# A two-layer decoder trunk on one core: where the first layer's weight sums are formed, where x's inverse root is computed, and a new order of units

## The chip, the core and the metric

The kernel runs on one core of a Trainium2 chip. The engines that matter are TensorE (PE in the profile; PEld is its weight load), VectorE (DVE), ScalarE (ACT) and GpSimd (POOL). SyncE (SP) and GpSimd issue DMAs. Each engine takes its instructions in the order in which they were emitted. SBUF holds data for all engines; PSUM receives the matmul results. The metric is the device time of one execution in microseconds (us), median of several.

## The reference

Two layers; in each, `h = RMSNorm(x)`, one projection `p = h @ W_in` (1024 to 3488 columns), four head groups on slices of `p`, each gated by a SiLU path, and an output projection added to `x`. All is float32, 512 tokens.

```python
h = rmsnorm(x, norm_g)
p = h @ w_in
(cq, ckv, kr, g_a, c_h, c_b, c_c, g_b, sg_u, sg_v, g_c, mq, mk, mv, g_d) = jnp.split(p, offs, axis=-1)
# A: latent attention from cq, ckv, kr   B: gated short convolution of c_c * c_h, times c_b
# C: sg_u times a causal mix of layernorm(sg_v)   D: block-sparse attention from mq, mk, mv
y = jnp.concatenate([o_a * silu(g_a), o_b * silu(g_b), o_c * silu(g_c), o_d * silu(g_d)], axis=-1)
x = x + y @ w_out
```

Two blocks of columns of `W_in` matter here: "sq" (`sg_v` and `mq`, 512 columns) and "kv" (`mk` and `mv`, 512 columns).

## The kernel before

**Precision.** A float32 product is made of three matmuls: each operand is split into a high part (rounded to the matmul type) and a low part (the rest), and high x high, high x low and low x high are summed in PSUM (`mm3`, L296). So each weight block of 128 x 1024 ("unit", 512 KB) is loaded as `raw`, its high part `whi` is copied from it, mostly on ScalarE, and its low part `wlo = raw - whi` is formed on VectorE from two SBUF tensors (`split_units` L455, `low_half` L497).

**Units and buffers.** All units of a layer are listed in order (`order`, from `SEQ0` for the first layer, L47, and `SEQ1` for the second, L50). `load_units` (L415) issues the loads on SyncE's queue in this order, `split_units` splits them in this order, and `main` (L1766) emits their matmuls. Raw blocks and low parts share a ring of eight buffers (`ringS`); a unit's low part goes to the ring buffer one before its raw block's. High parts have six buffers. A few units take other buffers that lie idle at that time: `hS` (two), `v4S` (four), `ydS` (two, idle until `mq` and `mk` take them, L1401). The first three units (`EARLY`) are split into the space of `yTh` and `yTl`, which is not yet used; in the profile p11's weights are therefore called yTh and yTl, and so are the row sums of the products below.

**Seven products instead of eight.** The token-major sq and kv columns are computed by a Strassen-like scheme: tokens in two halves, the 1024 inner rows in two halves, the columns in sq and kv. The four weight blocks are p11 and p21 (sq), p12 and p22 (kv), each of two units (j = 0, 1). The seven products of `SPROD` are p11, p21, p3, p4, p2, p1, p22; four of them use sums of weight blocks: p3 = p22 + p12, p1 = p12 + p11, p2 = p11 + p3, p4 = p21 + p2. `product` (L1834) emits 24 matmuls per product; p11 and p21 accumulate in the tiles pz, p3 and p4 in px, p2, p1 and p22 in py. `h_first`, `h_sums` and `sum_split` (L912 to L948) form the sums of rows of h that go with them, on VectorE (tiles `a`) with a split on ScalarE and VectorE. `p_out` (L1874) and its users take the results: `sv_chain` and `mqk_chain` for sq, `mqk_chain` and `mv_chain` for kv.

**Weight sums through DRAM.** For both layers the weight sums are formed by DMAs in DRAM (`t_sums`, L372): first eight copies, block to sum buffer, on SyncE's queue; then eight DMAs on GpSimd's queue that add a second block to the copy. Their results are then loaded as units p1 to p4 from `psum_w`. For the first layer this starts at 10 us of the plan (`TSP`), one step each 1.7 us (`PGAP`).

**Root of x.** In the first layer the norm's inverse root is not applied to h but to results. `x_stats` (L803) computes the mean square, at `ROWT` of the plan emits its power -0.5 on GpSimd (`pow_rstd`, L753), and splits it (`xr2`, the tile xr). `x_row` (L826) spreads it on GpSimd into two diagonal matrices (rdh, rdl), multiplies them by ones on PE (rrow), and copies the row to `rh`, by which the gates and features are scaled (`gate` L1223, `from_acc` L1293).

**Order of emission.** `Order` (L85) is a planner in Python: every chain of instructions is a generator, and each instruction is emitted when the planner's clocks of the engines say that its inputs are nearly there. The costs are fixed formulas in `Chain` (L177); GpSimd's is 290 ns plus 2.0 ns per element. Splits of units not yet wanted are held back while ScalarE's or VectorE's clock is more than `WSLACK` ahead. `TS0` is when the weight sums of the output projection and of the second layer start. `SGLOAD` names the product after which the spatial weights are loaded.

Of the kernel before, what the change touches and what calls it, by code (L numbers as in the profile page):

```python
# [29 lines left out]
TWO_PI = 6.283185307179586  # L30

NRING, NW, NT2 = 8, 6, 11
WSLACK = 100.0
AHEAD, URGENT, VSLACK = 4, 2, 300.0
NWARM, FILL, FILLEND = 6, 0.9, 15000.0
MIXT, MIXLAG, ROWT, COLT = 44000.0, 2000.0, 36000.0, 17500.0
KSPLIT, HMEAN = 6, 0.0
PAIRS = {}
LOPRIO = -5
# [4 lines left out]
STOK = (0, 1)  # L44
SPROD = ("p11", "p21", "p3", "p4", "p2", "p1", "p22")
SSUMS = {"p3": 0, "p2": 1, "p1": 2, "p22": 0}
SEQ0 = ['ga0', 'p11', 'p21', 'p3', 'p4', 'ga1', 'p2', 'p1', 'p22', 'ch0', 'su0', 'gc0', 'cc0', 'gd0', 'cb0', 'gd1', 'ch1', 'cc1', 'cb1', 'gb0', 'su1', 'gb1', 'gc1']  # L47
EARLY = [f"{n}{j}_0" if n in SPROD else f"{n}_0" for n in SEQ0[:3] for j in range(2 if n in SPROD else 1)][:3]
EARLYREL = EARLY[2][:-3] if EARLY[2][0] == "p" else EARLY[2][:-2]
SEQ1 = ['p11', 'ga0', 'p21', 'p3', 'p4', 'ga1', 'p2', 'ch0', 'p1', 'p22', 'cc0', 'gd0', 'gd1', 'su0', 'cb0', 'gb0', 'ch1', 'gc0', 'cc1', 'cb1', 'gb1', 'su1', 'gc1']  # L50
K0, K1, KK = (2, 3, 0, 1), (4, 5, 6, 7), (0, 2, 3, 1)
ZPROD = ("b11", "t3", "b21", "t4", "t2", "t1", "b22")
TS0 = 70000.0
NEWT = ((), ())
SUMLAT = 10000.0
HSTART = 'ga0'
FAR = 3
TSP, PGAP = 10000.0, 1700.0
HADD_G = ()
ZHOME = 'ss'  # L60
SGLOAD = ('p2', 'p4')
MLAGO = ('p4', 'p4')
TAIL = ((0, 256), (256, 512))

# [167 lines left out]
def hybrid_trunk(ctx: ExitStack, tc: tile.TileContext, x, positions, norm_g, w_c, w_f, w_t, w_o, mla_q_norm_g,  # L232
# [3 lines left out]
    V, A, G, PE = nc.vector, nc.scalar, nc.gpsimd, nc.tensor  # L236
# [125 lines left out]
    def z_src(l, n, j):  # L362
        return tsum[l, n][j] if n in ("t1", "t2", "t3", "t4") else quad(l, n, j)

    psum_w = {(l, n): dr.tile([2, P, 1024], F32, name=f"{n}_{l}") for l in STOK for n in ("p1", "p2", "p3", "p4")}
    tsum_ev.update({(l, n, j): Event() for l, n in psum_w for j in range(2)})

    def p_src(l, n, j):

        return psum_w[l, n][j] if len(n) == 2 else w_t[l, int(n[2]) - 1, 2 * int(n[1]) - 2 + j]  # L370

    def t_sums(*streams):  # L372

        first = streams[0][0] == 0 and streams[0][2] == "p"
        gap = PGAP if first else 4000.0 if len(streams) == 1 else 3000.0
        steps = [(l, src, t + n, b + x, y[0].replace("b", b).replace("t", t) + y[1:], j)
                 for n, x, y in (("3", "12", "b22"), ("1", "11", "b12"), ("2", "11", "t3"), ("4", "21", "t2"))
                 for l, src, t, b in streams for j in range(2)]
        for l, src, n, x, _, j in steps:
            o.clk["D"] = max(o.clk["D"], o.now) + 1500.0  # L380
            nc.sync.dma_start(src(l, n, j), src(l, x, j))
            yield o.now + gap
        for l, src, n, _, y, j in steps:
            o.clk["G"] = max(o.clk["G"], o.now) + 1000.0
            nc.gpsimd.dma_start(src(l, n, j), src(l, y, j), accum_op=ALU.add, max_dma_last_dim=1024)  # L385
            o.set(tsum_ev[l, n, j], o.now + (SUMLAT if first else 10000.0))
            yield o.now + gap

    FEATS = ["ga0", "ga1", "ch0", "ch1", "cb0", "cb1", "cc0", "cc1", "gb0", "gb1", "su0", "su1",
# [2 lines left out]
    for l in range(DEPTH):  # L392
# [18 lines left out]
        for half in range(2):  # L411
            for kq in WORDER:
                add_unit(w_o[l, half, kq], 2, 512, f"wo{half}{kq}_{l}")

    def load_units():  # L415
        for u in order:
            ch = Chain(o)
            u.raw_slots = ringS[u.idx % NRING]
            if u.name in ("uq_0", "ukv_0"):
                u.raw_slots = hS  # L420
                u.raw = yield from hS.get(ch, f"raw_{u.name}")
            elif u.name in ("p210_0", "p211_0"):
# [12 lines left out]
            key = (int(u.name[-1]), u.name[:-3], ord(u.name[-3]) - 48)
            if key in tsum_ev:
                yield from ch.wait(tsum_ev[key])
            n = u.a * u.b
            if u.name == "c0_0":
                for i in range(2):  # L440
                    sl = slice(i * n // 2, (i + 1) * n // 2)
                    ch = Chain(o)
                    dma(ch, P * n * 2, u.raw[:, sl], u.src[:, sl])
                    o.set(u.landed[i], ch.t)
                    if i == 0:
                        load_xk(1, 2)
            else:
                dma(ch, P * n * 4, u.raw[:, :n], u.src)
                ch.t += LATE.get(u.name, 0.0)
            o.set(u.loaded, ch.t)  # L450
            for e in LOAD_HOOKS.pop(u.name, ()):
                e()
            yield o.now
# [42 lines left out]

    def low_half(u, i, ch, raw, hi, g, whole):  # L497
        if u.lo is None and i == 0:
            u.lo = yield from ringS[(u.idx - 1) % NRING].get(ch, f"wlo_{u.name}", F32R)
            o.set(u.lo_got, o.now)  # L500
        yield from ch.wait(u.lo_got)
        n = u.a * u.b
        lo = u.lo[:, 0:n] if whole else u.lo[:, i * n // 2:(i + 1) * n // 2]
        while o.clk["V"] > o.now + VSLACK and u.idx > at[0] + URGENT:
            yield o.now + 100.0
        ch.t = max(ch.t, o.now)
        if g is None:
            yield from ch.dve(V.tensor_tensor, lo, raw, hi.bitcast(F32), op=ALU.subtract)
        else:
            yield from ch.dve(V.scalar_tensor_tensor, lo, in0=raw, scalar=g, in1=hi.bitcast(F32),  # L510
                              op0=ALU.mult, op1=ALU.subtract)
        o.set(u.half[i], ch.t)
        if whole:
            o.set(u.half[1], ch.t)
        if u.half[1 - i].t is not None:
            ch.t = max(ch.t, u.half[1 - i].t)
            u.raw_slots.put(ch)
            o.set(u.ready, ch.t)

    def drop(u, ch):  # L520

        if u.slots is not eS:
            u.slots.put(ch)
            ringS[(u.idx - 1) % NRING].put(ch)

    def unit(ch, name, half=None):
        u = units[name]
# [225 lines left out]
    def pow_rstd(ch, dst, src, n):  # L753
        return ch.pow(G.tensor_tensor, dst, src, nhalf[:, :n], op=ALU.pow)
# [48 lines left out]
    def x_stats():  # L803
        ch = Chain(o)
        for kp in range(KT // 2):
            yield from ch.wait(xk_ev[2 * kp + 1])
            for t in range(NT):
                yield from ch.act(A.activation, junk[:, 0:2 * P], xk[kp][:, t, :], AF.Square, scale=D ** -0.5,
                                  accum_out=xsum[:, t, kp:kp + 1])
            c2 = Chain(o, ch.t)  # L810
            yield from c2.wait(xk_tr[2 * kp + 1])
            v4S.put(c2)
        yield from ch.dve(V.tensor_reduce, xv[:, RV, :], xsum, axis=AX.X, op=ALU.add)
        yield from ch.dve(V.tensor_scalar, xv[:, RV, :], xv[:, RV, :], 1.0, EPS, op0=ALU.mult, op1=ALU.add)
        t0 = ch.t
        for i, f in ((RE, EPS), (REE, EPS * EPS)):
            yield from ch.dve(V.tensor_scalar, xv[:, i, :], xv[:, RV, :], f, None, op0=ALU.mult)
        o.set(v_ev, ch.t)
        c2 = Chain(o, max(t0, ROWT))
        yield from pow_rstd(c2, xv[:, RR, :], xv[:, RV, :], NT)  # L820

        yield from c2.dve(V.tensor_copy, xr2[:, 0, :], xv[:, RR, :])
        yield from c2.dve(V.tensor_tensor, xr2[:, 1, :], xv[:, RR, :], xr2[:, 0, :].bitcast(F32), op=ALU.subtract)
        o.set(r_ev, c2.t)
# [1276 lines left out]
    def start():  # L2101
# [40 lines left out]
        o.spawn(x_stats(), None, 5)  # L2142
        o.spawn(x_row(), ROWT, 5)
        o.spawn(main(), None, 10)
    o.spawn(t_sums((0, p_src, "p", "p")), TSP, 4)
    o.spawn(t_sums((0, z_src, "t", "b"), (1, p_src, "p", "p")), TS0, 4)
    o.spawn(start())
    o.run()
# [50 lines left out]
```

## Time and profile before

| | us |
|---|---|
| median of 3 runs | 500.29 |
| lowest, highest | 499.91, 501.26 |
| profiled execution, its own time | 498.24 |
| its span | 496.5 |
| VectorE busy | 415.7 |
| ScalarE busy | 341.5 |
| GpSimd busy | 127.4 |

The page lists busy time by engine and, in 40 slices of 12.4 us, the busy share in tenths. A row of the timeline has the start, the duration, the engine, the line, the operation, the tiles out<-in, a count, and in brackets how long the engine stood before it and what ended that. Nearly all rows of VectorE, ScalarE and GpSimd carry L189 and those of PE L219, the planner's emitters, so one goes by tiles. Tile names: raw_p, whi_p, wlo_p are the sq and kv units; a the row sums; Vt, K, Q, krt belong to group A; bst, bmv, vn to the layer norm of C; p<-p and p<-in_w_t_dram are the DMAs of `t_sums`.

### The profile page before, as it was taken

How to read it: one execution, taken by the hardware profiler on the slowest of the kernel's cores; microseconds unless marked ns; L12 is line 12 of the kernel's file. 1: busy time of each engine (PE TensorE's matmuls, PEld its weight loads, DVE VectorE, ACT ScalarE, POOL GpSimd, SP SyncE). 2: the span in 40 equal slices, each digit the busy share in tenths (PEclk: the TensorE clock that was granted, in tenths of full speed). 3: DMA queues.
4: the chain of work that ended last, by engine and by line, in shares of the span. 5: the costliest groups of instructions: out<-in, count | busy, mean ns of one | idle time of the engine just before them, and what ended most of it. 6: DMA issues, size and time to landing. Idle time of an engine off the chain costs nothing.

```text
span 496.5 us, 7502 instructions
## 1 busy us (share of the span) xinstructions
PE 479.1 (96%) x2408; PEld 405.8 (82%) x2408; DVE 415.7 (84%) x844; ACT 341.5 (69%) x894; POOL 127.4 (26%) x197
## 2 busy tenths in 40 slices
PE   8998589999999999999999999999999999999996
PEld 7986368787888888888889988888888888888885
DVE  3697579997898887989989768898899889997993
ACT  5896669788658865755767689887766767565450
POOL 8865490102074124200021111554123000000000
PEclk9999969999999999999999999999999999999999
DMA  8999974975589999558773259959952253226852
GB/s 266 410 192 329 157 254 159 368 307 212 178 165 243 265 265 240 134 186 290 262 269 138 60 203 338 352 173 234 246 114 65 84 154 122 86 66 218 297 225 86
DMA packets 45568, 104.43 MB, mean 210 GB/s; under 512 B 5958, under 2 KB 25752, under 8 KB 45016
## 3 DMA queue, kind: packets, MB, share of 16 engines
q1 hardware_dynamic: 27984, 86.77, 50.0%
q0 software_dynamic: 17440, 17.10, 21.9%
q8 instruction: 19, 0.31, 0.2%
q14 instruction: 21, 0.17, 0.1%
q10 hardware_dynamic: 104, 0.07, 0.1%
HBM read 96.07 MB, written 41.42 MB: 277 GB/s over the span
## 4 chain that ended last, share of the span: by engine, by line
PE 82%; DMA 10%; DVE 3%; POOL 1%; SPq 1%; issue 1%; ACT 1%; POOLq 0%; DVEq 0%
PE oy L219 6%; PE px L219 5%; PE py L219 5%; PE gc L219 5%; PE su L219 4%; PE gd L219 4%; PE gb L219 4%; PE cb L219 4%; PE ch L219 4%; PE cc L219 4%; PE oz L219 4%; PE ox L219 4%; PE cq L219 4%; PE sa L219 3%; DMA p<-in_w_t_dram 3%; PE pz L219 2%
## 5 line engine op out<-in xcount | busy, mean ns | idle before, releaser
L189 DVE TENSOR_TENSOR wlo_p<-raw_p,whi_p 128x1024 fp32r<-128x1024 f32 (+1 forms) x32 | 32.4, 1017 | 0.2 <-ACT whi_p L189 0.2
L189 ACT ACTIVATE whi_p<-raw_p 128x1024 fp32r<-128x1024 f32 (+1 forms) x30 | 26.5, 897 | 2.2 <-DMA raw_p<-p 2.2
L189 ACT ACTIVATE pa<-pa,mna 128x256 f32<-128x256 f32 (+3 forms) x49 | 25.7, 549 | 3.2 <-DVE mna L189 2.8
L189 ACT ACTIVATE phd<-pTd 128x512 fp32r<-128x512 f32 (+3 forms) x32 | 13.8, 436 | 19.8 <-PE pTd L219 19.8
L189 ACT ACTIVATE pd<-pd,mnd 128x128 f32<-128x128 f32 (+3 forms) x42 | 22.2, 543 | 4.3 <-DVE mnd L189 4.3
L189 ACT ACTIVATE pha<-pTa 128x512 fp32r<-128x512 f32 (+3 forms) x32 | 13.7, 434 | 14.6 <-PE pTa L219 14.5
L189 ACT ACTIVATE whi_t<-raw_t 128x1024 fp32r<-128x1024 f32 (+1 forms) x20 | 17.3, 879 | 6.1 <-DMA raw_t<-t 4.5
L219 PE MATMUL cq<-whi_c,hTh 128*128 128x416 f32 x64 | 20.6, 368 | 0.8 <-ACT hTh L189 0.8
L189 DVE CUSTOM_DVE_ANT_0 pd<-sd,maskb,rs_mq 128x256 f32<-128x256 f32 (+3 forms) x32 | 17.0, 544 | 4.1 <-PE pTd L219 3.7
L219 PE MATMUL cq<-whi_c,hTl 128*128 128x416 f32 x64 | 19.9, 356 | 0.3 <-DVE hTl L189 0.3
L219 PE MATMUL cq<-wlo_c,hTh 128*128 128x416 f32 x64 | 20.0, 358 | 0.0
L189 DVE TENSOR_TENSOR wlo_t<-raw_t,whi_t 128x1024 fp32r<-128x1024 f32 (+1 forms) x20 | 19.9, 1002 | 0.0
L219 PE MATMUL py<-whi_p,yTh 128*128 128x512 f32 x48 | 19.2, 400 | 0.3 <-DVE x L189 0.3
L189 DVE CUSTOM_DVE_ANT_0 pa<-sa,maskb,rs_q 128x512 f32<-128x512 f32 (+3 forms) x32 | 16.8, 545 | 2.6 <-PE sa L219 1.9
L219 PE MATMUL py<-whi_p,yTl 128*128 128x512 f32 x48 | 18.8, 391 | 0.0
L219 PE MATMUL py<-wlo_p,yTh 128*128 128x512 f32 x48 | 18.7, 390 | 0.0
L189 DVE TENSOR_TENSOR pla<-pTa,pha 128x512 fp32r<-128x512 f32 (+3 forms) x32 | 15.3, 485 | 3.4 <-ACT pha L189 3.3
L189 DVE TENSOR_TENSOR pld<-pTd,phd 128x512 fp32r<-128x512 f32 (+3 forms) x32 | 15.2, 485 | 2.2 <-ACT phd L189 1.9
L189 POOL TENSOR_SCALAR xss<-xss 128x1 f32<-128x1 f32 x4 | 2.6, 646 | 54.4 <-ACT jk L189 49.0
L189 POOL TENSOR_TENSOR ms<-ms,nhalf 128x2 f32<-128x2 f32 x8 | 8.5, 1069 | 29.5 <-DVE ms L189 24.0
L385 POOL DMA_DIRECT2D t<-t x8 | 9.5, 1408 | 25.6 <-DMA t<-t 15.2
L219 PE MATMUL pTa<-ident,pa 128*128 128x128 f32 x80 | 14.2, 275 | 1.2 <-ACT mix L189 1.2
(474 smaller groups left out, 1869.5 us busy)
## 6 DMA issues: line engine op xcount, KB each, us to landing
p<-in_w_t_dram SPq DMA_DIRECT2D x16, 512.0 KB, 7.3
raw_p<-p SPq DMA_DIRECT2D x16, 512.0 KB, 5.9
t<-in_w_o_dram SPq DMA_DIRECT2D x16, 512.0 KB, 7.2
raw_t<-t SPq DMA_DIRECT2D x16, 512.0 KB, 6.1
raw_p<-in_w_t_dram SPq DMA_DIRECT2D x12, 512.0 KB, 5.2
raw_b<-in_w_o_dram SPq DMA_DIRECT2D x12, 512.0 KB, 4.2
p<-in_w_t_dram POOLq DMA_DIRECT2D x8, 512.0 KB, 15.9
p<-p POOLq DMA_DIRECT2D x8, 512.0 KB, 12.2
```

The lines of the kernel that those rows point to most:

```text
L189: f(*a, **k)
L219: f(*a, **k)
L385: nc.gpsimd.dma_start(src(l, n, j), src(l, y, j), accum_op=ALU.add, max_dma_last_dim=1024)
```

## The change

- The first layer's sums p1 to p4 are no longer made by `t_sums` in DRAM. `chip_sums(j)`, one chain for each j, loads p12's block into a `ydS` buffer and forms the sums on GpSimd in place in SBUF: p3 = p22 + p12 in p22's raw buffer, p1 = p12 + p11 in the yd buffer, p2 = p11 + p3 in p11's raw buffer once p11 is split, p4 = p21 + p2 in p21's raw buffer once p21 is split. That is eight additions of 128 x 1024.
- `load_units` no longer loads p1, p2 and p4; under p3's name it loads p22's block, into `hS`. p11's and p21's raw buffers are held past their split, and p3's until p2 has read it (`low_half`). p210's low part goes to another ring buffer (`low_home`).
- x's inverse root is computed on VectorE by `newton_rstd` (ten small operations and a copy), and is planned at 24 instead of 36 us.
- `SEQ0`: p2 follows p4 directly, then ch0, ga1, p1, p22; some later units change places too.
- `WSLACK` 100 to 600, `TS0` 70 to 80 us, `SGLOAD` of the first layer p2 to p3. The second layer's sums are still made by `t_sums`.

```diff
--- before.py
+++ after.py
@@ -30,10 +30,10 @@
 TWO_PI = 6.283185307179586
 
 NRING, NW, NT2 = 8, 6, 11
-WSLACK = 100.0
+WSLACK = 600.0
 AHEAD, URGENT, VSLACK = 4, 2, 300.0
 NWARM, FILL, FILLEND = 6, 0.9, 15000.0
-MIXT, MIXLAG, ROWT, COLT = 44000.0, 2000.0, 36000.0, 17500.0
+MIXT, MIXLAG, ROWT, COLT = 44000.0, 2000.0, 24000.0, 17500.0
 KSPLIT, HMEAN = 6, 0.0
 PAIRS = {}
 LOPRIO = -5
@@ -44,21 +44,20 @@
 STOK = (0, 1)
 SPROD = ("p11", "p21", "p3", "p4", "p2", "p1", "p22")
 SSUMS = {"p3": 0, "p2": 1, "p1": 2, "p22": 0}
-SEQ0 = ['ga0', 'p11', 'p21', 'p3', 'p4', 'ga1', 'p2', 'p1', 'p22', 'ch0', 'su0', 'gc0', 'cc0', 'gd0', 'cb0', 'gd1', 'ch1', 'cc1', 'cb1', 'gb0', 'su1', 'gb1', 'gc1']
+SEQ0 = ['ga0', 'p11', 'p21', 'p3', 'p4', 'p2', 'ch0', 'ga1', 'p1', 'p22', 'su0', 'cc0', 'gc0', 'cb0', 'gd0', 'gb0', 'ch1', 'cc1', 'gd1', 'cb1', 'su1', 'gb1', 'gc1']
 EARLY = [f"{n}{j}_0" if n in SPROD else f"{n}_0" for n in SEQ0[:3] for j in range(2 if n in SPROD else 1)][:3]
 EARLYREL = EARLY[2][:-3] if EARLY[2][0] == "p" else EARLY[2][:-2]
 SEQ1 = ['p11', 'ga0', 'p21', 'p3', 'p4', 'ga1', 'p2', 'ch0', 'p1', 'p22', 'cc0', 'gd0', 'gd1', 'su0', 'cb0', 'gb0', 'ch1', 'gc0', 'cc1', 'cb1', 'gb1', 'su1', 'gc1']
 K0, K1, KK = (2, 3, 0, 1), (4, 5, 6, 7), (0, 2, 3, 1)
 ZPROD = ("b11", "t3", "b21", "t4", "t2", "t1", "b22")
-TS0 = 70000.0
+TS0 = 80000.0
 NEWT = ((), ())
-SUMLAT = 10000.0
 HSTART = 'ga0'
 FAR = 3
 TSP, PGAP = 10000.0, 1700.0
 HADD_G = ()
 ZHOME = 'ss'
-SGLOAD = ('p2', 'p4')
+SGLOAD = ('p3', 'p4')
 MLAGO = ('p4', 'p4')
 TAIL = ((0, 256), (256, 512))
 
@@ -362,17 +361,41 @@
     def z_src(l, n, j):
         return tsum[l, n][j] if n in ("t1", "t2", "t3", "t4") else quad(l, n, j)
 
-    psum_w = {(l, n): dr.tile([2, P, 1024], F32, name=f"{n}_{l}") for l in STOK for n in ("p1", "p2", "p3", "p4")}
+    psum_w = {(l, n): dr.tile([2, P, 1024], F32, name=f"{n}_{l}") for l in STOK if l for n in ("p1", "p2", "p3", "p4")}
     tsum_ev.update({(l, n, j): Event() for l, n in psum_w for j in range(2)})
 
     def p_src(l, n, j):
 
+        if l == 0 and len(n) == 2:
+            n = {"p1": "p12", "p2": "p11", "p3": "p22", "p4": "p21"}[n]
         return psum_w[l, n][j] if len(n) == 2 else w_t[l, int(n[2]) - 1, 2 * int(n[1]) - 2 + j]
 
+    def chip_sums(j):
+
+        ch = Chain(o)
+        u1, u2, u3, u4, u11, u21 = (units[f"{n}{j}_0"] for n in ("p1", "p2", "p3", "p4", "p11", "p21"))
+        u3.kept = Event()
+        u1.raw_slots, u1.raw = ydS, (yield from ydS.get(ch, f"raw_{u1.name}", [P, 1024], F32))
+        dma(ch, P * 4096, u1.raw, u1.src)
+        yield from ch.wait(u3.landed[0])
+        yield from ch.pool(G.tensor_tensor, u3.raw, u3.raw, u1.raw, op=ALU.add)
+        o.set(u3.loaded, ch.t)
+        yield from ch.wait(u11.loaded)
+        yield from ch.pool(G.tensor_tensor, u1.raw, u1.raw, u11.raw, op=ALU.add)
+        o.set(u1.loaded, ch.t)
+        yield from ch.wait(u11.ready)
+        u2.raw, u2.raw_slots = u11.raw, u11.raw_slots
+        yield from ch.pool(G.tensor_tensor, u2.raw, u2.raw, u3.raw, op=ALU.add)
+        o.set(u3.kept, ch.t)
+        yield from ch.wait(u21.ready)
+        u4.raw, u4.raw_slots = u21.raw, u21.raw_slots
+        yield from ch.pool(G.tensor_tensor, u4.raw, u4.raw, u2.raw, op=ALU.add)
+        o.set(u4.loaded, ch.t)
+        o.set(u2.loaded, ch.t)
+
     def t_sums(*streams):
 
-        first = streams[0][0] == 0 and streams[0][2] == "p"
-        gap = PGAP if first else 4000.0 if len(streams) == 1 else 3000.0
+        gap = 4000.0 if len(streams) == 1 else 3000.0
         steps = [(l, src, t + n, b + x, y[0].replace("b", b).replace("t", t) + y[1:], j)
                  for n, x, y in (("3", "12", "b22"), ("1", "11", "b12"), ("2", "11", "t3"), ("4", "21", "t2"))
                  for l, src, t, b in streams for j in range(2)]
@@ -383,7 +406,7 @@
         for l, src, n, _, y, j in steps:
             o.clk["G"] = max(o.clk["G"], o.now) + 1000.0
             nc.gpsimd.dma_start(src(l, n, j), src(l, y, j), accum_op=ALU.add, max_dma_last_dim=1024)
-            o.set(tsum_ev[l, n, j], o.now + (SUMLAT if first else 10000.0))
+            o.set(tsum_ev[l, n, j], o.now + 10000.0)
             yield o.now + gap
 
     FEATS = ["ga0", "ga1", "ch0", "ch1", "cb0", "cb1", "cc0", "cc1", "gb0", "gb1", "su0", "su1",
@@ -412,8 +435,16 @@
             for kq in WORDER:
                 add_unit(w_o[l, half, kq], 2, 512, f"wo{half}{kq}_{l}")
 
+    SUM0 = [f"{n}{j}_0" for n in ("p1", "p2", "p4") for j in range(2)]
+    HELD0 = [f"{n}{j}_0" for n in ("p11", "p21") for j in range(2)]
+
+    def low_home(u):
+        return (u.idx - (3 if u.name == "p210_0" else 1)) % NRING
+
     def load_units():
         for u in order:
+            if u.name in SUM0:
+                continue
             ch = Chain(o)
             u.raw_slots = ringS[u.idx % NRING]
             if u.name in ("uq_0", "ukv_0"):
@@ -422,6 +453,9 @@
             elif u.name in ("p210_0", "p211_0"):
                 u.raw_slots = v4S
                 u.raw = yield from v4S.get(ch, f"raw_{u.name}", [P, D], F32)
+            elif u.name in ("p30_0", "p31_0"):
+                u.raw_slots = hS
+                u.raw = yield from hS.get(ch, f"raw_{u.name}")
             elif u.name[:-3] in SPROD and u.name[-3] == "1" and u.name not in ("p111_0", "p221_0"):
                 u.raw_slots = hS
                 u.raw = yield from hS.get(ch, f"raw_{u.name}")
@@ -447,7 +481,7 @@
             else:
                 dma(ch, P * n * 4, u.raw[:, :n], u.src)
                 ch.t += LATE.get(u.name, 0.0)
-            o.set(u.loaded, ch.t)
+            o.set(u.landed[0] if u.name in ("p30_0", "p31_0") else u.loaded, ch.t)
             for e in LOAD_HOOKS.pop(u.name, ()):
                 e()
             yield o.now
@@ -496,7 +530,7 @@
 
     def low_half(u, i, ch, raw, hi, g, whole):
         if u.lo is None and i == 0:
-            u.lo = yield from ringS[(u.idx - 1) % NRING].get(ch, f"wlo_{u.name}", F32R)
+            u.lo = yield from ringS[low_home(u)].get(ch, f"wlo_{u.name}", F32R)
             o.set(u.lo_got, o.now)
         yield from ch.wait(u.lo_got)
         n = u.a * u.b
@@ -514,14 +548,18 @@
             o.set(u.half[1], ch.t)
         if u.half[1 - i].t is not None:
             ch.t = max(ch.t, u.half[1 - i].t)
+            o.set(u.ready, ch.t)
+            if u.name in HELD0:
+                return
+            if u.name in ("p30_0", "p31_0"):
+                yield from ch.wait(u.kept)
             u.raw_slots.put(ch)
-            o.set(u.ready, ch.t)
 
     def drop(u, ch):
 
         if u.slots is not eS:
             u.slots.put(ch)
-            ringS[(u.idx - 1) % NRING].put(ch)
+            ringS[low_home(u)].put(ch)
 
     def unit(ch, name, half=None):
         u = units[name]
@@ -817,7 +855,8 @@
             yield from ch.dve(V.tensor_scalar, xv[:, i, :], xv[:, RV, :], f, None, op0=ALU.mult)
         o.set(v_ev, ch.t)
         c2 = Chain(o, max(t0, ROWT))
-        yield from pow_rstd(c2, xv[:, RR, :], xv[:, RV, :], NT)
+        yield from c2.dve(V.tensor_copy, xv[:, RR, :], xv[:, RV, :])
+        yield from newton_rstd(c2, xv[:, RR, :])
 
         yield from c2.dve(V.tensor_copy, xr2[:, 0, :], xv[:, RR, :])
         yield from c2.dve(V.tensor_tensor, xr2[:, 1, :], xv[:, RR, :], xr2[:, 0, :].bitcast(F32), op=ALU.subtract)
@@ -2142,7 +2181,8 @@
         o.spawn(x_stats(), None, 5)
         o.spawn(x_row(), ROWT, 5)
         o.spawn(main(), None, 10)
-    o.spawn(t_sums((0, p_src, "p", "p")), TSP, 4)
+    for j in range(2):
+        o.spawn(chip_sums(j), TSP + j * PGAP, 4)
     o.spawn(t_sums((0, z_src, "t", "b"), (1, p_src, "p", "p")), TS0, 4)
     o.spawn(start())
     o.run()
```

## The prediction

> **What bounds the kernel now.** First the page: the busy line, and the slices for a place where the bounding engine rests.
>
> ```profile
> span 496.5 us, 7502 instructions
> ...
> PE 479.1 (96%) x2408; PEld 405.8 (82%) x2408; DVE 415.7 (84%) x844; ACT 341.5 (69%) x894; POOL 127.4 (26%) x197
> ...
> PE   8998589999999999999999999999999999999996
> ```
>
> PE is busy for 96% of the span, so only its gaps can be won, and one slice (5, at 50 to 62 us) is a gap. Next the matmul engine in order of time around that slice; the bracket is PE's idle time before the row and what ended it.
>
> ```profile
> 47.88 0.50 PE L219 MATMUL pz<-yTh,hTh 128*128 128x512 f32 x1 [1.99 <-DVE Vt L189]
> ...
> 55.27 0.39 PE L219 MATMUL pz<-whi_p,hTl 128*128 128x512 f32 x1
> 60.49 0.79 PE L219 MATMUL rrow<-rdh,ones 128*128 128x512 f32 x1 [4.83 <-POOL rdh L189]
> 62.64 0.79 PE L219 MATMUL rrow<-rdl,ones 128*128 128x512 f32 x1 [1.35 <-POOL rdl L189]
> ...
> 66.17 0.80 PE L219 MATMUL px<-whi_p,yTh 128*128 128x512 f32 x1 [1.46 <-ACT yTh L189]
> ```
>
> PE stands in unit p11 (47.88), then in p21 behind rrow, a matmul of x's root that needs rdh and rdl from GpSimd. Unit p3 (px) starts at 66.17. The same block of 48 matmuls (p3, p4) stands in the chain of waits once per layer:
>
> ```profile
> 66.17 12.98 PE px L219 x48
> ...
> 304.60 10.88 PE px L219 x48
> ```
>
> The first is 2.10 us longer: it begins at a reduced clock. A 512-column matmul at full rate is 10.88 / 48 = 0.227 us. From 55.27 to 66.17 are 10.90 us for six such (one pz, two rrow, three pz left of p21), 1.36 us; 9.54 us are lost. With the 1.99 that is **11.5 us, and 13.6 with the clock**. Why rdh came late is in GpSimd's order of time:
>
> ```profile
> 44.68 1.43 POOL L189 TENSOR_TENSOR xv<-xv,nhalf 128x4 f32<-128x4 f32 x1
> ...
> 54.79 1.01 POOL L385 DMA_DIRECT2D p<-p  x1 [7.10 <-DMA p<-p]
> ...
> 59.40 1.04 POOL L189 TENSOR_TENSOR rdh<-ident,xr 128x512 fp32r<-128x512 f32 x1
> ```
>
> L385 is an accumulating DMA of t_sums: GpSimd stood 7.10 us for the one before it, with rdh behind. And VectorE waited too, for x's root on GpSimd (ahead of Vt) and for pz:
>
> ```profile
> 46.14 0.20 DVE L189 CAST xr<-xv 128x4 fp32r<-128x4 f32 x1 [3.25 <-POOL xv L189]
> ...
> 64.75 0.43 DVE L189 BATCH_NORM_STATS2 bst<-pz 128x6 f32<-128x256 f32 x1 [7.79 <-PE pz L219]
> ```
>
> That is 3.25 + 7.79 = 11.04 us of idle VectorE. Last the busy times by stretch:
>
> ```profile
> core 0: us, PE busy (x) PEld busy (x) DVE busy (x) ACT busy (x) POOL busy (x), PEclk, DMA share, GB/s
> 35.00:66.00 31.00, 21.53 (x89) 16.52 (x87) 19.21 (x45) 18.03 (x72) 17.61 (x26) 0.90 1.04 245
> ...
> 66.20:79.20 13.00, 13.00 (x50) 10.54 (x50) 12.54 (x27) 11.36 (x34) 9.28 (x5) 0.85 0.44 165
> 79.20:110.00 30.80, 30.52 (x146) 25.26 (x145) 30.26 (x56) 26.07 (x77) 2.92 (x5) 1.00 0.90 332
> ```
>
> Before p3 VectorE is busy 19.21 of 31 us; from p3 to 110 us both VectorE (42.80 of 43.80) and PE are full. So PE's 11.5 us are worth only what VectorE can follow.
>
> **What goes.** In the first layer the eight DRAM copies and eight accumulating DMAs of t_sums go, and with them GpSimd's 7.10 us wait; also four of the fourteen weight loads of the sq and kv units. DMA share in 35 to 66 falls from 1.04; what is late next is no transfer but the sums themselves. The root's power (1.43 us on GpSimd) becomes a copy and ten small VectorE operations, emitted 12 us earlier by the plan (ROWT).
>
> ```profile
> 35.20 0.35 DVE L189 TENSOR_SCALAR ms<-ssq,xv 128x2 f32<-128x2 f32 x2
> ```
>
> Two dependent small ones take 0.35 us with an end that overlaps the next; about 0.14 us each, so 11 x 0.14 = 1.5 us of VectorE, at a time when it has no gap to hide them. rdh and rdl then stand ahead of the adds, which must wait for p22's block.
>
> **What comes.** Eight GpSimd adds of 128x1024. No row has one. The nearest are rdh, 1.04 us for 512 columns, and a 128-column one:
>
> ```profile
> 29.08 0.40 POOL L189 TENSOR_TENSOR rope_scratch<-rope_scratch,ones 128x128 f32<-128x128 f32 x1
> ```
>
> Slope (1.04 - 0.40) / 384 = 1.67 ns a column gives 1.9 us; doubling rdh gives 2.08. I take 1.9: 8 x 1.9 = 15.2 us (at most 16.6). GpSimd was busy 17.61 of 31 us here, partly in its DMA rows, so it has the room.
>
> The cost lies elsewhere: **GpSimd and VectorE hold each other up.** Six rows, three operations, each alone and beside the other engine:
>
> ```profile
> 74.21 1.27 POOL L189 COPY K<-krt 128x512 f32<-128x512 f32 x1
> ...
> 294.98 0.61 POOL L189 COPY K<-krt 128x512 f32<-128x512 f32 x1 [2.88 <-DVE krt L189]
> ...
> 74.92 1.10 DVE L189 TENSOR_TENSOR K<-K,rs_k 128x512 f32<-128x512 f32 x1
> ...
> 77.42 0.68 DVE L189 TENSOR_TENSOR K<-K,rs_k 128x512 f32<-128x512 f32 x1
> ...
> 27.72 0.47 DVE L189 SCALAR_TENSOR_TENSOR wlo_ukv<-raw_ukv,pcol,whi_ukv 128x256 fp32r<-128x256 f32 x1
> ...
> 29.56 0.75 DVE L189 SCALAR_TENSOR_TENSOR wlo_ukv<-raw_ukv,pcol,whi_ukv 128x256 fp32r<-128x256 f32 x1
> ```
>
> The copy is 0.66 us longer beside VectorE, VectorE's K 0.42 longer beside the copy, wlo_ukv 0.28 longer while a GpSimd operation runs. All three VectorE operations read two SBUF tensors. How much of VectorE's work before p3 is of that kind, by its groups from 35 to 66 us:
>
> ```profile
> L189 DVE TENSOR_TENSOR wlo_p<-raw_p,whi_p 128x1024 fp32r<-128x1024 f32 x4 | 4.9, 1218 | 0.0
> L189 DVE TENSOR_TENSOR a<-hTh,hTl 128x512 f32<-128x512 f32 x7 | 4.8, 679 | 0.0
> L189 DVE TENSOR_TENSOR a<-a,a 128x512 f32<-128x512 f32 x6 | 4.1, 681 | 0.0
> ...
> L189 DVE TENSOR_TENSOR yTl<-raw_p,yTh 128x1024 fp32r<-128x1024 f32 x1 | 1.2, 1214 | 0.0
> ...
> L189 DVE SCALAR_TENSOR_TENSOR krt<-ct,ms,gr_b 128x32 f32<-128x32 f32 x4 | 0.9, 238 | 0.0
> ```
>
> 15.9 us; the view's sixteen groups sum to 23.4 (their ends overlap), so 0.68 of VectorE's work conflicts. The share f of the adds' 15.2 us that VectorE pays: at its old busy share (19.21 / 31 = 0.62) 0.62 x 0.68 = 0.42; with no idle left 0.68; nothing if the adds fall in gaps; 1 if every add stops it. I take 0.42, nearest to what the rows measure: 6.4 us.
>
> [...]
>
> ```profile
> 66.29 3.34 POOL L189 TENSOR_TENSOR rs_q<-rs_q,nhalf 128x16 f32<-128x16 f32 x1
> ...
> 67.31 0.68 DVE L189 TENSOR_TENSOR yTl<-a,yTh 128x512 fp32r<-128x512 f32 x1
> ```
>
> VectorE read two SBUF tensors at its usual 0.68 us inside that power: it is held while GpSimd reads, which an add does nearly throughout. [...]
>
> **Moves and new waits.** The adds wait in GpSimd's queue for p22's block, which follows the last reads of raw_uq and raw_ukv, since they free its buffers:
>
> ```profile
> 25.98 0.60 DVE L189 SCALAR_TENSOR_TENSOR wlo_uq<-raw_uq,pcol,whi_uq 128x384 fp32r<-128x384 f32 x1
> ...
> raw_p<-in_w_t_dram SPq DMA_DIRECT2D x12, 512.0 KB, 5.2
> ```
>
> 26.6 and (wlo_ukv) 30.3 plus 5.2 us: first add 32 to 36 us. Behind it stand ms's powers, which Vt needs, and behind Vt p11's second PSUM bank. mq now waits for a yd buffer until p1's raw weights are split; ScalarE has its squares behind it, and p21's two banks stay taken. Cover: mq's root was only wanted late.
>
> ```profile
> 112.66 2.91 POOL L189 TENSOR_TENSOR rs_mq<-rs_mq,nhalf 128x16 f32<-128x16 f32 x1 [12.30 <-DVE rs_mq L189]
> ```
>
> So nothing; if the cover goes, ScalarE stands for some us behind mq, which is in the range. The unit order changes no matmul; p2 comes 5.4 us sooner, p1 and p22 later, which gives their sums time: 0, within 1 us both ways. WSLACK, SGLOAD and TS0 move splits, one load and the later layer's DMA sums, all under a full PE: 0, within 1.5 us both ways.
>
> **Sum**, against the profiled execution (span 496.5, its own time 498.24): p3 waits for VectorE, so its start moves by -11.04 + 1.5 + 6.4 = -3.1 us, to 63.0. With short stalls the block runs at full clock, -2.1. Together **-5.2 us: 493.0**. The timed median is 500.29, 2.05 above the profiled time; the change taken from it gives **495.1**. Times below are on that scale.
>
> **Rivals.**
> - *The adds are nearly free* (f under 0.25, 3.8 us). For: GpSimd's queue is empty of waits, ScalarE and PSUM-fed work lies between. Against: 0.68. Then -5.7 - 2.1 gives 492.5; at f = 0 PE's own limit, -13.6, gives 486.7.
> - *The change doesn't do what it says: rrow or VectorE stops PE as before.* If rdh falls behind the adds, or f is 0.63 (9.5 us, the idle that was there less the root), p3 starts at 66 again: 500.3. For: the same idle can be spent only once.
> - *Slower: VectorE in turn with GpSimd.* While GpSimd has adds queued, each two-input operation of VectorE, be it krt's 0.24 us, waits a whole add. [...] Place: 37 to 62 us, where krt stands ahead of Vt and Vt ahead of pz. Then p3 is 3.4 us late, and the clock is not regained: 503.7; with f = 1, 506.0. It decides from 9.5 us of waiting, about six adds fully paid. Against: K's 0.42 us, and that the adds with p21 come after p3's.
> - *p4's sums come last.* From 35.5 us, 15.2 of adds, about 6 of other GpSimd work and eight waits of 0.6 end at 62, p4's split 2 later; p4 is due 5.4 after p3. It bites only if p3 starts before 58.6, and then leaves about 491.
>
> **How the numbers follow.** A run of this kernel can tell 0.3%, 1.5 us. Forecast (f 0.25 to 0.68, 492.5 to 498.8): 0.38. Adds nearly free, p4's sums included (486.7 to 492.5): 0.22. As before (498.8 to 501.8): 0.18. Slower in turn (501.8 to 506.0): 0.22. So faster 0.60, same 0.18, slower 0.22. The forecast's own range is 492.5 to 498.8; the 8 in 10 runs from 488 (0.05 below) to 503.7 (about 0.10 above).
>
> **What would show it.** Right: no DMA row on GpSimd before 80 us; rrow without a wait on rdh; px starting near 63 and taking about 10.9 us; wlo_p or a rows on VectorE stretched by 0.5 to 1.9 us beside GpSimd adds of 1.9 us or more; no 3.25 us before xr. Wrong: unstretched rows (nearly free); Vt or krt late and PE idle at p11 (slower); PE waiting for whi_p of p4 (late sums). A gap after 80 us, from mq's wait or the new order, would be a cause I have priced at nothing.

## The result and the profile after

The changed kernel took 505.3 us (median of 4 runs, 504.41 to 505.52) beside 500.29 for the kernel before on the same chip (median of 3; a fourth execution of it took 795.24 us and counts in no comparison): a ratio of 1.009 between the means, 95% interval 1.007 to 1.012, **slower by 0.9%**. The profiled run took 505.52 us, 7.3 more than the one before (498.24). The forecast was 495.1.

First the page of the changed kernel: the span, the busy line and PE's slices.

```profile
span 503.8 us, 7481 instructions
...
PE 482.2 (96%) x2408; PEld 408.8 (81%) x2408; DVE 432.7 (86%) x854; ACT 338.4 (67%) x867; POOL 144.3 (29%) x196
...
PE   9986688999999999999999999999999999999997
```

PE's one dip (the 5) has become two 6s and two 8s from 38 to 88 us, earlier and longer. VectorE is busy 432.7 us instead of 415.7. PE in order of time (the bracket is idle time before the row and what ended it):

```profile
36.65 0.44 PE L218 MATMUL q<-whi_uq,cTl 128*128 128x384 f32 x1 [1.33 <-DVE cTl L188]
...
42.93 0.69 PE L218 MATMUL q<-whi_uq,cTl 128*128 128x384 f32 x1 [3.93 <-DVE cTl L188]
...
55.39 0.69 PE L218 MATMUL q<-whi_uq,cTh 128*128 128x384 f32 x1 [5.70 <-DVE Vt L188]
...
69.44 0.39 PE L218 MATMUL px<-whi_p,yTh 128*128 128x512 f32 x1
...
72.37 0.50 PE L218 MATMUL px<-whi_p,yTl 128*128 128x512 f32 x1 [1.71 <-DVE yTl L188]
...
74.09 0.39 PE L218 MATMUL rrow<-rdh,ones 128*128 128x512 f32 x1
...
77.66 0.50 PE L218 MATMUL px<-whi_p,yTl 128*128 128x512 f32 x1 [1.82 <-DVE yTl L188]
```

The wait that the change was to remove is gone: rrow runs without any. (It also stands later in PE's order, in p3 instead of p21, but rdl, ready at 67.3 us, would have been in time for its old place, just before 68.8.) But every wait shown is now on VectorE, 1.33 + 3.93 + 5.70 + 1.71 + 1.82 = 14.5 us, where the four rows of before had 9.63. Unit p3 (px) starts at 69.44 instead of 66.17. The matmul after p4 starts at 87.14 us instead of 78.97, with the same 316 matmuls done, and after 77.66 PE has no wait over 0.8 us up to 130 us. So the whole loss, 7.3 us in these two executions, is made here. What held VectorE, in its order of time:

```profile
36.59 2.73 DVE L188 TENSOR_SCALAR ms<-ssq,xv 128x2 f32<-128x2 f32 x2
...
39.84 2.30 DVE L188 TENSOR_SCALAR ms<-ssq,xv 128x2 f32<-128x2 f32 x1
...
48.54 2.33 DVE L188 SCALAR_TENSOR_TENSOR newton<-newton,xv 128x4 f32<-128x4 f32 x1
...
51.26 2.45 DVE L188 TENSOR_TENSOR a<-hTh,hTl 128x512 f32<-128x512 f32 x1
...
57.45 2.38 DVE L188 SCALAR_TENSOR_TENSOR krt<-ct,ms,gr_b 128x32 f32<-128x32 f32 x1
```

and GpSimd's rows, with the adds (raw_p from two raw_p):

```profile
30.73 2.97 POOL L188 TENSOR_TENSOR raw_p<-raw_p,raw_p 128x1024 f32<-128x1024 f32 x1 [6.17 <-DMA raw_p<-in_w_t_dram]
...
36.90 5.21 POOL L188 TENSOR_TENSOR raw_p<-raw_p,raw_p 128x1024 f32<-128x1024 f32 x2
...
45.69 7.46 POOL L188 TENSOR_TENSOR raw_p<-raw_p,raw_p 128x1024 f32<-128x1024 f32 x3
57.06 2.72 POOL L188 TENSOR_TENSOR raw_p<-raw_p,raw_p 128x1024 f32<-128x1024 f32 x1 [3.91 <-issue]
60.55 1.04 POOL L188 TENSOR_TENSOR rdh<-ident,xr 128x512 fp32r<-128x512 f32 x1 [0.77 <-PE kv L218]
```

Lay the two lists over each other. Taken one by one, these adds end at 33.7, 39.3, 42.1, 48.1, 50.8, 53.2 and 59.8 us. Each of the VectorE rows lies in a stretch of adds and ends where one of them ends, or its own 0.5 us later (a). An operation on two columns, 0.2 us of work, stands there for 2.3. All eight adds in the page's group (busy total, mean ns):

```profile
L188 POOL TENSOR_TENSOR raw_p<-raw_p,raw_p 128x1024 f32<-128x1024 f32 x8 | 20.8, 2610 | 11.9 <-DMA raw_p<-in_w_t_dram 6.2
```

They take 2.61 us each, not the 1.9 that was assumed (from 2.35 to 2.97).

### The profile page after: what moved, and what is told of

Its sections match the earlier page's. It is cut to its first block, busy times and chain, and to the rows that moved or that the text cites. A ratio compares the mean times of both kernels' runs of the same rounds, so it can differ in the third digit from the quotient of the medians.

```text
span 503.8 us, 7481 instructions
## 1 busy us (share of the span) xinstructions
PE 482.2 (96%) x2408; PEld 408.8 (81%) x2408; DVE 432.7 (86%) x854; ACT 338.4 (67%) x867; POOL 144.3 (29%) x196
## 4 chain that ended last, share of the span: by engine, by line
PE 87%; DVE 9%; ACT 1%; issue 1%
PE py L218 7%; PE oy L218 6%; PE cq L218 5%; PE su L218 4%; PE gd L218 4%; PE cb L218 4%; PE cc L218 4%; PE gc L218 4%; PE gb L218 4%; PE ch L218 4%; PE oz L218 4%; PE ox L218 4%; PE px L218 4%; PE ga L218 3%; PE sa L218 3%; DVE a L188 2%
## 5 line engine op out<-in xcount | busy, mean ns | idle before, releaser
L188 ACT ACTIVATE pa<-pa,mna 128x384 f32<-128x384 f32 (+3 forms) x47 | 24.9, 551 | 3.1 <-DVE mna L188 2.9
L188 ACT ACTIVATE pha<-pTa 128x512 fp32r<-128x512 f32 (+3 forms) x32 | 13.9, 434 | 18.6 <-PE pTa L218 18.4
L188 POOL TENSOR_TENSOR raw_p<-raw_p,raw_p 128x1024 f32<-128x1024 f32 x8 | 20.8, 2610 | 11.9 <-DMA raw_p<-in_w_t_dram 6.2
L188 DVE TENSOR_TENSOR pla<-pTa,pha 128x512 fp32r<-128x512 f32 (+3 forms) x32 | 15.4, 484 | 1.8 <-ACT pha L188 1.7
L188 POOL MEMSET kl0d<- 64x512 f32 x4 | 2.1, 522 | 47.0 <-DVE yaa L188 37.0
```

The lines of the kernel that those rows point to most:

```text
L188: f(*a, **k)
```

## Experiments

The theory after the result: each add stops VectorE for most of its length, and PE follows VectorE. The rivals: the new order or the root's new place loses the time; GpSimd is merely busy and its other work is late; the waits for the buffers' loads do it. Ratios below are to the kernel before, run on the same chip.

### Fewer adds that matter: one column, and half of them

In the first kernel each add works on one column; in the second only those of j = 1 do. Both keep the plan's cost of a whole add (2338 ns), so the order of work on every engine is that of the changed kernel. The other columns of the sums are left out. Below is the second kernel's line, where `W` is 1024 for j = 0 and 1 for j = 1; the first has 1 in its place everywhere.

```diff
-        yield from ch.pool(G.tensor_tensor, u3.raw, u3.raw, u1.raw, op=ALU.add)
+        yield from ch._emit("G", 2338.0, G.tensor_tensor, (u3.raw[:, 0:W], u3.raw[:, 0:W], u1.raw[:, 0:W]), dict(op=ALU.add))
...
```

> The changed kernel with each of the eight GpSimd adds cut to the first of its 1024 columns (the sums p1 to p4 of the first layer are left out but for that column); the order of every engine is the changed kernel's. Theory A (the adds' reads hold VectorE): the 15 us by which VectorE's busy time grew go, p3 starts near 56 instead of 70 us, 489 to 492 us. Rival B (the new order, the held buffers and the new waits cost the time): nothing changes, 503 to 506 us. Rival C (the adds' length in GpSimd's own queue, ahead of ms and rdh): as A, 489 to 493.

> The changed kernel with the four adds of j = 1 cut to one column (those sums are left out but for it), the four of j = 0 whole; the order of every engine is the changed kernel's. Theory A: each whole add costs VectorE about 2 us and the time is the middle of 505.3 (eight) and 489.4 (none), 495 to 500 us. Rival (there is slack for some of the adds, and only the last few cost): under 493 or over 502 us.

One column everywhere: 489.36 us, ratio 0.977 (0.974 to 0.980). Half of the adds whole: 496.64, ratio 0.993 (0.990 to 0.995). With 1.009 for all eight, four adds are worth 1.6% each time, **2.0 us an add**. The busy lines of the two pages, the one-column kernel first:

```profile
PE 475.2 (98%) x2408; PEld 403.9 (83%) x2408; DVE 417.3 (86%) x854; ACT 337.6 (69%) x867; POOL 125.6 (26%) x196
```

```profile
PE 477.9 (96%) x2408; PEld 404.8 (82%) x2408; DVE 425.3 (86%) x854; ACT 338.1 (68%) x867; POOL 134.5 (27%) x196
```

VectorE runs the same 854 instructions in 417.3, 425.3 and 432.7 us: 8.0 us for four adds, 15.4 for eight. That is 1.9 us of VectorE an add, 0.74 of the adds' 20.8 us. The same VectorE rows as above, in the one-column kernel:

```profile
34.23 0.52 DVE L188 TENSOR_SCALAR ms<-ssq,xv 128x2 f32<-128x2 f32 x2
...
35.26 0.22 DVE L188 TENSOR_SCALAR ms<-ssq,xv 128x2 f32<-128x2 f32 x1
...
40.72 0.16 DVE L188 SCALAR_TENSOR_TENSOR newton<-newton,xv 128x4 f32<-128x4 f32 x1
...
41.25 0.68 DVE L188 TENSOR_TENSOR a<-hTh,hTl 128x512 f32<-128x512 f32 x1
```

The four rows that took 2.73, 2.30, 2.33 and 2.45 us beside whole adds take 0.52, 0.22, 0.16 and 0.68. And its px starts 13.0 us earlier, the matmul after p4 17.6 us (69.54 against 87.14):

```profile
56.39 0.39 PE L218 MATMUL px<-whi_p,yTh 128*128 128x512 f32 x1
```

### GpSimd as busy, but reading nothing

Each add becomes two memsets of its 128x1024 target. The sums are left out; the order is that of the changed kernel.

```diff
-        yield from ch.pool(G.tensor_tensor, u3.raw, u3.raw, u1.raw, op=ALU.add)
+        yield from ch._emit("G", 2338.0, lambda t: (G.memset(t, 0.0), G.memset(t, 0.0)), (u3.raw,), {})
...
```

> The changed kernel with each add replaced by two memsets of the same 128x1024 block, about 2.1 us together (the sums p1 to p4 of the first layer are left out: zeros): GpSimd is as long busy but reads nothing. Theory A: VectorE's two-input operations keep their usual time and only its one-input copies are stretched, 490 to 495 us. Rival C (GpSimd's queue): as the changed kernel, 500 to 505 us. Rival B: 503 to 506 us.

It took 491.31 us, ratio 0.982 (0.979 to 0.984), within 2 us of the one-column kernel, and VectorE is busy 417.8 us (417.3 there). GpSimd's rows and then VectorE's beside them:

```profile
30.08 1.97 POOL L381 MEMSET raw_p<- 128x1024 f32 x2 [4.93 <-DVE ct L188]
...
35.30 1.96 POOL L381 MEMSET raw_p<- 128x1024 f32 x2
```

```profile
31.06 2.34 DVE L188 TENSOR_TENSOR yTl<-raw_p,yTh 128x1024 fp32r<-128x1024 f32 x2
...
35.01 1.26 DVE L188 TENSOR_SCALAR ms<-ssq,xv 128x2 f32<-128x2 f32 x1
...
36.02 0.27 DVE L188 TENSOR_SCALAR ms<-ssq,xv 128x2 f32<-128x2 f32 x1
...
36.41 0.88 DVE L188 TENSOR_TENSOR a<-hTh,hTl 128x512 f32<-128x512 f32 x1
```

Two-input yTl, the first of its two beside memsets, takes 1.17 us each, and wlo_p at 43.56 us, wholly beside memsets, takes 1.21 (1.22 in the one-column kernel). So a busy GpSimd is not the cause: against the one-column kernel, 8 x 1.97 us of memsets cost 2 us and 8 x 2.61 us of adds 16. What the adds do and the memsets don't is read, and that leaves the reads. One ms of 1.26 us beside a memset, against 0.22 in the one-column kernel, shows that writes aren't wholly free.

### The same adds, on VectorE, in the same places

```diff
-        yield from ch.pool(G.tensor_tensor, u3.raw, u3.raw, u1.raw, op=ALU.add)
+        yield from ch._emit("G", 2338.0, V.tensor_tensor, (u3.raw, u3.raw, u1.raw), dict(op=ALU.add))
...
```

> The eight adds of the change run on VectorE instead of GpSimd, each put into VectorE's queue at the point of the plan where GpSimd's add was issued; the order of every other instruction on every engine is that of the changed kernel. Theory (GpSimd's add holds VectorE for about 2 us each, 16 us in all; the kernel with one-column adds took 489.4 us): an add costs VectorE only its own 1.2 us, 8 x 1.2 = 9.7, so 497 to 501 us, VectorE's small sums (ms, krt, newton) unstretched. Rival (the adds' waits for weight loads are what hurts, and would now stop VectorE's own queue): 502 to 508, with VectorE rows that waited for raw_p from a DMA for 3 us or more.

496.97 us, ratio 0.993 (0.991 to 0.995), at the lower edge of the theory's range: the whole computation, 1.6% faster than the changed kernel and **0.7% faster than the kernel before**. VectorE's rows:

```profile
34.23 1.22 DVE L188 TENSOR_TENSOR raw_p<-raw_p,raw_p 128x1024 f32<-128x1024 f32 x1
...
35.90 0.35 DVE L188 TENSOR_SCALAR ms<-ssq,xv 128x2 f32<-128x2 f32 x2
```

An add done by VectorE takes it 1.22 us; one done for it by GpSimd took 1.9 us of its time. The rows of ms are back at 0.35. The loads' waits are no cause either: they stand in VectorE's own queue now, and no row of it from 28 to 76 us waited over 0.3 us.

### The adds in pieces

Eight GpSimd pieces of 128 columns, back to back in the add's place and with its planned cost.

```diff
+        yield from ch._emit("G", 2338.0, lambda a, b: [G.tensor_tensor(a[:, c:c + 128], a[:, c:c + 128], b[:, c:c + 128], op=ALU.add) for c in range(0, 1024, 128)], (u3.raw, u1.raw), {})
...
```

> Each add of the change cut into eight GpSimd pieces of 128 columns, issued back to back at the add's own place, so that the order of the other engines is that of the changed kernel. Theory, hold by the instruction (VectorE's operation waits for the piece that runs, about 0.45 us, and the next piece for it): small VectorE operations stretched by at most 0.5 us, VectorE's whole wait less than with whole adds, but GpSimd's own time 29 instead of 21 us, so 496 to 503. Rival, hold by the queue (GpSimd keeps its place from piece to piece): ms and krt stretched by 2 us or more as with whole adds, 506 to 514.

510.92 us, ratio 1.022 (1.019 to 1.025). The time is the rival's; the rows are the theory's but for one. VectorE is busy 425.6 us, 8.3 more than with one column, where whole adds made it 15.4. Two of its rows:

```profile
35.77 0.92 DVE L188 TENSOR_SCALAR ms<-ssq,xv 128x2 f32<-128x2 f32 x2
...
52.98 0.45 DVE L188 SCALAR_TENSOR_TENSOR krt<-ct,ms,gr_b 128x32 f32<-128x32 f32 x1
```

GpSimd, and the PE row that pays:

```profile
31.30 6.31 POOL L381 TENSOR_TENSOR raw_p<-raw_p,raw_p 128x128 f32<-128x128 f32 x8 [5.45 <-ACT cTh L188]
...
57.31 11.04 POOL L388 TENSOR_TENSOR raw_p<-raw_p,raw_p 128x128 f32<-128x128 f32 x16
68.32 3.32 POOL L392 TENSOR_TENSOR raw_p<-raw_p,raw_p 128x128 f32<-128x128 f32 x8
```

```profile
72.69 0.80 PE L218 MATMUL rrow<-rdh,ones 128*128 128x512 f32 x1 [4.79 <-POOL rdh L188]
```

Most VectorE operations wait for one piece at most (krt 0.45, not 2.38). But a piece waits for VectorE too: 3.32 / 8 = 0.42 us while VectorE is idle, 6.31 / 8 = 0.79 beside it. All the pieces take 39.6 us (6.31 + 5.31 + 3.77 + 6.52 + 11.04 + 2 x 3.32), not the 29 that were expected. GpSimd falls behind, and rdh, ms and their readers with it. The row that doesn't fit:

```profile
72.60 3.32 POOL L392 TENSOR_TENSOR raw_p<-raw_p,raw_p 128x128 f32<-128x128 f32 x8
```

```profile
73.76 3.61 DVE L188 TENSOR_TENSOR rs_k<-rs_k,e 128x16 f32<-128x16 f32 x1 [7.80 <-ACT junk L188]
```

rs_k takes 0.26 us in the changed kernel. Here it stood from inside the eight pieces and ended at 77.37 us, when rdl behind them was done too (76.92), while the pieces kept their 0.42 us each. So VectorE is not let in after every piece, and for this row the rival is right; what decides it is not shown. In this run the hold works both ways, and the shorter instructions only shift the bill: 510.92 us against 505.3 with whole adds.

### Other ways to form the sums, with a plan of their own

Here the planner is told of each operation's own engine and cost, and orders anew: VectorE adds; pieces planned at 400 ns each; accumulating DMAs into SBUF.

```diff
-        yield from ch.pool(G.tensor_tensor, u3.raw, u3.raw, u1.raw, op=ALU.add)
+        yield from ch.dve(V.tensor_tensor, u3.raw, u3.raw, u1.raw, op=ALU.add)
```

```diff
+        for c in range(0, 1024, 128):
+            yield from ch._emit("G", 400.0, G.tensor_tensor, (u3.raw[:, c:c + 128], u3.raw[:, c:c + 128], u1.raw[:, c:c + 128]), dict(op=ALU.add))
```

```diff
+            o.clk["G"] = max(o.clk["G"], ch.t, o.now) + 1000.0
+            nc.gpsimd.dma_start(dst, src, accum_op=ALU.add)
+            ch.t = o.clk["G"] + SUMLAT
...
```

> The changed kernel with the eight adds on VectorE instead of GpSimd, 1.13 us each, 9 us of VectorE in place of about 16 of waiting. Theory A: 497 to 501 us, better than the changed kernel. Rival (VectorE is bound either way, and its plan now puts the adds ahead of what PE needs): 503 to 507 us.

> The changed kernel with each add cut into eight of 128 columns, on GpSimd. Theory A with a port that is taken for one instruction: a VectorE operation waits at most one piece, 0.3 to 0.4 us, instead of a whole add, so small operations (ms, krt, the steps of the root) lose most of their wait: 493 to 500 us. Rival (the port is taken for the same sum of time, whatever the pieces): 503 to 508 us.

> The changed kernel with each add replaced by an accumulating DMA into the same SBUF buffer, from p12 and p11 in DRAM for p3 and p1, from SBUF for p2 and p4. Theory A: no engine reads the port, so VectorE is not held: 489 to 494 us. Rival (GpSimd stands in its queue for one DMA before it issues the next, as in the kernel before, with rdh and ms behind): 497 to 503 us.

They took 506.06 us, ratio 1.012 (1.008 to 1.016); 525.04, 1.051 (1.046 to 1.055); and 527.26, 1.055 (1.051 to 1.058). All three missed. The port that two of these expectations speak of was the author's assumption; the runs show which rows are held and for how long, and no port. One PE row of each shows what a new order did, in this order of kernels:

```profile
47.35 0.80 PE L218 MATMUL pz<-yTh,hTh 128*128 128x512 f32 x1 [4.32 <-DVE Vt L188]
```

```profile
87.31 0.80 PE L218 MATMUL px<-whi_p,hTh 128*128 128x512 f32 x1 [12.46 <-ACT whi_p L188]
```

```profile
92.03 0.80 PE L219 MATMUL px<-whi_p,hTh 128*128 128x512 f32 x1 [18.15 <-ACT whi_p L189]
```

In the last two, p4's sums come 12 to 18 us late. In the third kernel GpSimd stood 8.79 us for one accumulating DMA before it issued the next (81.17 us), as its rival said, and PE had already stood 11.43 us for rdl. In the first, Vt is late at p11 and there are waits as far as 86 us. These runs test the planner as much as the adds, and say little on the theory: the 9 us between the two kernels with VectorE adds (506.06 and 496.97) are the plan's, which also moved work between ScalarE and VectorE (ScalarE is busy 343.7 us in the first, 338.3 in the second).

### The change's other parts, in the kernel before

The root alone (the diff's ROWT and its lines of x_stats); the order alone (its SEQ0, WSLACK, TS0, SGLOAD); and the root with rdh and rdl on VectorE too. All three keep the sums in DRAM.

```diff
+        yield from c2.dve(V.tensor_copy, xv[:, RR, :], xv[:, RV, :])
+        yield from newton_rstd(c2, xv[:, RR, :])
```

```diff
+SEQ0 = ['ga0', 'p11', 'p21', 'p3', 'p4', 'p2', 'ch0', 'ga1', 'p1', 'p22', 'su0', 'cc0', 'gc0', 'cb0', 'gd0', 'gb0', 'ch1', 'cc1', 'gd1', 'cb1', 'su1', 'gb1', 'gc1']
```

```diff
-            yield from ch.pool(G.tensor_tensor, d[i].rearrange("p (t c) -> p t c", t=NT),
+            yield from ch.dve(V.tensor_tensor, d[i].rearrange("p (t c) -> p t c", t=NT),
```

> The kernel before with only the root of x on VectorE and planned at 24 us; the sums stay in DRAM. Theory A: the stall of the kernel before was rdh behind the accumulating DMAs, so PE's 4.83 us at rrow and VectorE's 3.25 us at xr go: 491 to 495 us. Rival (the sums through DRAM are late anyway, or VectorE cannot follow): 498 to 501 us.

> The kernel before with only the new order of units, WSLACK 600, TS0 80 us and the earlier load of the spatial weights. Theory A: these cost and gain little, 499 to 502 us, and p3 still waits for rrow. Rival B (the order costs the time): 503 to 506 us.

> The kernel before with its sums in DRAM; only x's root (as Newton steps) and the two products rdh and rdl go to VectorE, so that nothing that PE waits for stands behind GpSimd's accumulating DMA. Theory (what PE lost before p3 was rdh behind that DMA, 4.83 and 1.35 us, and the root's move alone did not bring it forward): PE waits for rrow under 1 us, VectorE 1.4 us more, 495 to 499. Rival (sinT, which waits behind the same DMA, or PSUM held by rrow takes the place of rdh): 500 to 504, with a VectorE row that waited 3 us or more for sinT.

503.48 us, ratio 1.007 (1.004 to 1.010); 505.88, 1.010 (1.006 to 1.013); 507.94, 1.015 (1.012 to 1.018). None came as its theory said: the order alone lies in its rival's range, the other two lie above both of theirs. One cause stands in front of all three. GpSimd and PE with the root alone:

```profile
56.35 1.02 POOL L385 DMA_DIRECT2D p<-p  x1 [9.06 <-DMA p<-p]
...
63.33 1.04 POOL L189 TENSOR_TENSOR rdh<-ident,xr 128x512 fp32r<-128x512 f32 x1
```

```profile
64.42 0.79 PE L219 MATMUL rrow<-rdh,ones 128*128 128x512 f32 x1 [5.08 <-POOL rdh L189]
```

With the accumulating DMAs in GpSimd's queue, rdh stands behind one that waited 9.06 us for the DMA before it, though the root is planned at 24 instead of 36 us. With rdh and rdl on VectorE, sinT does, as that run's rival said, and VectorE stands for it with rdl behind:

```profile
63.15 0.30 DVE L189 TENSOR_TENSOR rbk<-krt,sinT 128x64 f32<-128x64 f32 x1 [5.42 <-POOL sinT L189]
```

With the order alone PE waits longer for rdh, and then for p2's sums:

```profile
62.08 0.79 PE L219 MATMUL rrow<-rdh,ones 128*128 128x512 f32 x1 [7.67 <-POOL rdh L189]
...
83.43 0.50 PE L219 MATMUL py<-whi_p,yTh 128*128 128x512 f32 x1 [2.67 <-ACT yTh L189]
```

So neither part gains without the sums in SBUF. Whether the old order would do with the sums in SBUF stays open: built that way, the program ran for only 139.91 us, which can't be the whole work, and its time says nothing.

## Why the prediction was wrong

- **What bounds the kernel: right.** PE's gaps before p3 were 11.5 us, and the DMA wait on GpSimd with rdh behind it made the largest of them: without it rrow waits for nothing, and no accumulating DMA stands on GpSimd before 80 us.
- **All terms but one: their sum was right, partly by luck.** Without the adds' cost the prediction's -11.04 + 1.5 - 2.1 = -11.6 gives 500.3 - 11.6 = 488.7. The one-column kernel measured 0.977 x 500.3 = 488.8 (487.5 to 490.1). So the idle VectorE, the root's price (VectorE is busy 417.3 - 415.7 = 1.6 us longer) and the moves at nothing hold as a sum; each alone was not measured with the sums in SBUF. px starts at 56.39 us, where these terms give 66.17 - 11.04 + 1.5 = 56.6. The block behind it runs at full clock (1.00 granted from 55.5 to 79.2 us) but stands 1.52 us for yTl, which no term held, so most of the 2.1 us is spent again. Between the two profiled executions the gain is 498.24 - 488.3 = 9.9 us, not 11.6.
- **The step that failed** is "The share f of the adds' 15.2 us that VectorE pays ... I take 0.42, nearest to what the rows measure: 6.4 us". Measured: 15.4 us. Two factors were off. The length was 20.8 us in place of 15.2, so at 0.42 the term would have been 8.7; the share was 0.74, which makes it 15.4. The term is 9.0 us too small: 495.1 + 9.0 = 504.1, and without the clock's 2.1, 506.2. Measured: 505.3. The clock was not regained: 0.91 was granted from 70 to 88 us, 1.00 in the one-column kernel. The place differs from the sum's: p3 would start at 63.0 + 9.0 = 72.0 us and starts at 69.44; the rest is paid inside p3 (1.71 + 1.82).
- **Why the share was too low.** It multiplied VectorE's busy share by that of its two-input work, as if operations met the adds at random. But the held rows did not pass by: krt, 0.25 us in the one-column kernel, took 2.38 and ended with its add (59.83 and 59.78 us), so that it paid the rest of the add. And the rows of ms, which the share left out, were held too (2.30 against 0.22 us). One of the six rows was also misread: wlo_ukv's 0.47 us at 27.72 was not alone, but inside a GpSimd row of 1.34 us (27.12, rope_scratch) that takes 0.40 by itself. There GpSimd was the one held.
- **The rival *VectorE in turn with GpSimd* was right** in mechanism, and nearly in place: krt is held as it says and Vt comes late behind such rows, and p3 starts at 69.44 where it has 66.17 + 3.4 = 69.6; but PE pays at q and p3 rather than at p11. That its size (503.7 to 506.0) fits is partly luck: its adds were too short (1.9 against 2.61 us) and its share too high. Its 3.4 us are 12.9 us of waiting less the 9.5 that had been idle, and the 12.9 was the author's estimate, 1.6 of each add's 1.9 us (12.8 if multiplied out). No run shows the 0.3 us an add that it leaves VectorE; measured are 15.4 of the adds' 20.8 us, 0.74, where it has 12.9 of 15.2, or all. It had 0.22; the argument against it, K's 0.42 us, came from a short copy (0.61 us alone), after which VectorE had little left to wait for.
- **VectorE "is held while GpSimd reads": borne out, but not for reads alone.** The adds read and took 505.3 us; the memsets of the same blocks read nothing and took 491.3. ms was held by the adds (2.30 us against 0.22) and once, for 1.26 us, beside a memset.
- **The adds' length.** The slope's 1.9 us was too short: the shortest add took 2.35. The slope came from rows of other operands, rdh with a broadcast one; the 128-column row was near (0.40, and 0.42 for a piece).
- **rdh "ahead of the adds": wrong, without harm.** It stands behind seven of them at 60.55, and in the one-column kernel too (46.64), so this is the plan's order. It is 13.9 us later than there because VectorE, itself held, finished the root late (xr at 60.23); rrow is only needed at 74.09.
- **p4's sums last: did not happen.** PE reaches p4 without a wait.

## What to carry to other kernels

GpSimd was no free place here for an elementwise operation that reads SBUF, with VectorE busy for 84% of the span before: the adds cost VectorE 15.4 of their 20.8 us. Before such a move, price the operation at up to its whole length on VectorE (0.74 of it here), and if VectorE does it faster than that, leave it there (here 1.2 against 1.9 us each, 1.6% of the kernel). A share of conflicting work is the wrong measure where one engine stops the other until it is done, as the adds did krt (2.38 against 0.25 us); ask instead whether VectorE will have any such operation ready during each GpSimd instruction. In a planned order, change one engine's work without changing the order before you judge it: the same adds on VectorE gave 497 or 506 us.

## What was not expected of the hardware

VectorE's TENSOR_SCALAR on two columns was held by GpSimd's add (2.30 against 0.22 us) like newton, an operation of two inputs (2.33 against 0.16). The hold is mutual: 128-column adds on GpSimd took 0.42 us with VectorE idle and 0.79 in the mean of eight beside it. In one row it did not end with one instruction: a VectorE operation of 0.26 us stood 3.61 us beside a row of such adds. And much of what was held so long was small: four rows of 0.16 to 0.68 us account for 8.2 of the 15.4 us (2.73 + 2.30 + 2.33 + 2.45 less 0.52, 0.22, 0.16 and 0.68).
